# 64-slot experts: the second half of each column block turned by transposes instead of a fold product

## The chip, the cores and the metric

One core of one Trainium2 chip runs the whole kernel. TensorE is called PE here, VectorE DVE, ScalarE ACT, as in the profile's rows; SP issues the loads. The metric is device time in microseconds (us), the median of several runs; beside it stands one profiled execution, from which all rows come.

## The reference

A two-layer decoder trunk on 256 tokens of 1024 channels. Each layer mixes tokens (two attentions) and then channels; the second layer's channel mixer is a top-2-of-8 mixture of experts, and the change lies there:

```python
def _swiglu(x, w1, w3, w2):
    return (jax.nn.silu(x @ w1) * (x @ w3)) @ w2
...
    logits = (xt @ w_router).astype(jnp.float32)
    top_v, top_e = lax.top_k(logits, TOP_K)
    gates = jax.nn.softmax(top_v, axis=-1)
...
    def run(args):
        xb, e = args
        return _swiglu(xb, w1[e], w3[e], w2[e])
```

Everything is float32; w1 and w3 are 1024 x 3584, w2 is 3584 x 1024 for each expert.

## The kernel before

The eight experts are ranked by load and run as four pairs; in each pair one expert gets 128 token slots (large) and one gets 64 (small). Both are worked on in column blocks of the hidden width 3584: three blocks of 1024 columns and one of 512, that is seven parts of 512 columns. `plan` writes the order of steps out by hand. One step is one 1 MB tile of weights. For each block the steps are: w1 of the large, w1 of the small, w3 of the large, w3 of the small expert ("up", 4 steps each, 2 in the block of 512), then w2 ("down") of the block before, small and then large. There are 336 steps, 84 in a pair.

A step passes four engines. SP loads the tile into `raw` (L95, six buffers). ACT casts it to the rounded high part `whi` (L1135, five buffers). DVE subtracts the two to get the low part `wlo` (L1143, four buffers); that frees `raw` for a later load. PE multiplies with both: twelve 512-wide matmuls in a step of a large expert (L119 to L121), eight in one of a small expert (L1080, L1081). `run` casts four steps ahead for `whi` and three for `wlo`. Other work is hung between the steps: `mid[s]` runs before step s's casts, `end[s]` after its matmuls. Each engine works its list in that order.

With 64 slots a small expert would leave half of PE's columns unused, so its two operand parts stand side by side: slots 0 to 63 hold the product with the high part of the tokens, 64 to 127 that with the low part, and the two halves of the result have to be added. The up products of a part stay 128 x 512 in PSUM (`mps`), and `lift` copies them to SBUF (`mh`, four buffers, L1270). Later the part is turned so that the hidden columns become the contraction of w2: `turn_pe` multiplies each 128 x 128 square with `fold`, two identity matrices of 64 on top of each other, which turns it and adds its halves in one product (`ftp`, L1295). `turn_silu` then takes the Silu of the w1 side into `fs` (L1306), `turn_mult` multiplies with the w3 side (L1311), and `turn_small` splits the result into high and low part `sh` (L127, L128). A large expert's part is only turned, with transposes (`htp`, L1299).

The turn of a small expert's block stands after the last w2 step of its block before. In the second, third and fourth pair the work that closes the previous pair falls beside it: `acc_split` (`yh`, `yl`) and `combine`, which scatters the expert's rows back (`cbp`, L1348, L1349) and adds them to `x` (L1352): four parts in a row for the small expert of the previous pair, at the first turn, and spread over several steps for the large one, around the second.

Of the kernel before, what the change touches and what calls it, by code (L numbers as in the profile page):

```python
# [10 lines left out]
F32 = mybir.dt.float32  # L11
# [4 lines left out]
AF = mybir.ActivationFunctionType  # L16
OP = mybir.AluOpType
# [28 lines left out]
LCAP, SCAP = 128, 64  # L46
# [32 lines left out]
class Net:  # L79
# [1205 lines left out]
    def turn_pe(self, hid, turn, bi):  # L1285
        nc = self.nc
        small = self.jobs[self.blocks[bi][0]][2]
        hs = hid.pop(bi)
        turn[bi] = {"ps": []}
        for n in range(self.blocks[bi][2] // 512):  # L1290
            if small:
                ps = self.mmp.tile([128, 2, 4, SCAP], F32, name="ftp", tag="mm")
                for a in range(2):
                    for q in range(4):
                        nc.tensor.matmul(ps[:, a, q, :], hs[a][n][:, q * 128:(q + 1) * 128], self.fold, start=True, stop=True)  # L1295
            else:
                ps = self.mmp.tile([128, 4, 128], F32, name="htp", tag="mm")
                for q in range(4):
                    nc.tensor.transpose(ps[:, q, :], hs[n][:, q * 128:(q + 1) * 128], self.ident)  # L1299
            turn[bi]["ps"].append(ps)  # L1300

    def turn_silu(self, turn, bi):
        turn[bi]["s"] = []
        for ps in turn[bi]["ps"]:
            s = self.mp.tile([128, 4, SCAP], F32, name="fs", bufs=2)
            self.nc.scalar.activation(s, ps[:, 0], AF.Silu)  # L1306
            turn[bi]["s"].append(s)

    def turn_mult(self, turn, bi):
        for s, ps in zip(turn[bi]["s"], turn[bi]["ps"]):  # L1310
            self.nc.vector.tensor_tensor(s, s, ps[:, 1], op=OP.mult)  # L1311

    def turn_small(self, turn, bi):
        hh = self.mp.tile([128, 2, 4, 128], F32R, name="sh")
# [127 lines left out]
```

## Time and profile before

| | us |
|---|---|
| runs | 1671.28, 1671.52, 1675.92 (median 1671.52) |
| the profiled execution | 1670.91 |
| its span, first to last instruction | 1669.1 |
| stretch of the expert stage that the rows cover | 806 to 1637 |
| granted clock of PE, mean over the span | 0.986 |

The profiled execution's own time is 1.8 us above its span. Engine shares of the page are averages over two layers with different limits; what concerns the change is in the expert stage.

### The profile page before, as it was taken

The page shows a single profiled execution, that of the slowest core. Times are in us where ns is not written, and L with a number is a line of the kernel's source. Part 1 is how long each engine was busy: PE and PEld are TensorE (multiplying, and loading weights), DVE is VectorE, ACT ScalarE, POOL GpSimd, SP SyncE. Part 2 cuts the span into 40 slices and gives each one's busy share as a digit, 9 for nine tenths or more (in the row PEclk, how much of TensorE's full clock was granted, in tenths as well). Part 3 has the DMA queues.
Part 4 walks back from the last instruction along what each step waited for, and adds up shares of the span by engine and source line. Part 5 has one row for each costly group of instructions (what it writes and reads, how often), then busy time and mean ns, then how long its engine had stood idle before and what let it go on. Part 6 is the DMA issues. An engine that isn't in the chain of part 4 may idle for free. (4 is left out here: it accounts for less than half of the span.)

```text
span 1669.1 us, 22506 instructions
## 1 busy us (share of the span) xinstructions
PE 1617.4 (97%) x8152; PEld 1343.1 (80%) x8152; DVE 1380.3 (83%) x1686; ACT 1137.4 (68%) x1366; POOL 43.5 (3%) x40
## 2 busy tenths in 40 slices
PE   8899999999989999989999999999999999999996
PEld 7788787888879887878788887888887888878884
DVE  6997777554567668769899899999999999999997
ACT  5546644443436657538787888878887888787874
POOL 0331000000000000000000000000000000000000
PEclk9999999999989999999999999999999999999998
DMA  7533455655536444538999999999999999999993
GB/s 242 180 117 125 157 186 174 211 186 179 182 122 223 137 156 139 195 109 304 400 401 409 398 409 409 403 403 397 408 409 401 403 403 404 409 404 408 406 397 129
DMA packets 171585, 481.26 MB, mean 288 GB/s; under 512 B 8876, under 2 KB 33592, under 8 KB 171464
## 3 DMA queue, kind: packets, MB, share of 16 engines
q1 hardware_dynamic: 170120, 474.98, 75.9%
q0 software_dynamic: 1344, 4.75, 0.9%
q8 instruction: 66, 1.08, 0.3%
q14 instruction: 55, 0.45, 0.1%
HBM read 478.65 MB, written 1.05 MB: 287 GB/s over the span
## 5 line engine op out<-in xcount | busy, mean ns | idle before, releaser
L1143 DVE TENSOR_TENSOR wlo<-raw,whi 128x2048 fp32r<-128x2048 f32 (+1 forms) x338 | 753.4, 2272 | 29.2 <-ACT whi L1135 20.5
L1135 ACT CAST whi<-raw 128x2048 fp32r<-128x2048 f32 (+1 forms) x338 | 637.7, 1905 | 127.4 <-DMA raw<-in_expert_w_dram 57.1
L107 DVE TENSOR_TENSOR wlo<-raw,whi 128x1024 fp32r<-128x1024 f32 (+2 forms) x218 | 254.7, 1190 | 149.0 <-issue 79.0
L105 ACT CAST whi<-raw 128x1024 fp32r<-128x1024 f32 (+2 forms) x222 | 218.4, 1015 | 178.4 <-PE hps L121 51.7
L119 PE MATMUL mps<-wlo,g 128*128 128x512 f32 x448 | 177.8, 397 | 6.8 <-DVE x L1352 3.5
L1080 PE MATMUL mps<-wlo,g 128*128 128x512 f32 x448 | 177.4, 396 | 0.0
L121 PE MATMUL mps<-whi,g 128*128 128x512 f32 x448 | 177.3, 396 | 0.0
L120 PE MATMUL mps<-whi,g 128*128 128x512 f32 x448 | 176.3, 393 | 0.0
L1081 PE MATMUL mps<-whi,g 128*128 128x512 f32 x448 | 175.9, 393 | 0.0
L119 PEld LDWEIGHTS mps<-wlo,g 128*128 128x128 f32 x448 | 84.5, 189 | 27.7 <-DVE x L1352 4.8
L121 PEld LDWEIGHTS mps<-whi,g 128*128 128x128 f32 x448 | 84.4, 188 | 20.2
L120 PEld LDWEIGHTS mps<-whi,g 128*128 128x128 f32 x448 | 84.5, 189 | 19.5
L1080 PEld LDWEIGHTS mps<-wlo,g 128*128 128x128 f32 x448 | 84.1, 188 | 18.7
L1081 PEld LDWEIGHTS mps<-whi,g 128*128 128x128 f32 x448 | 84.1, 188 | 18.6
L402 PE MATMUL dqp<-x,whi 128*128 128x512 f32 x256 | 95.6, 414 | 2.2 <-DVE vm L486 2.2
L119 PE MATMUL macc<-wlo,hi 128*128 128x512 f32 x224 | 89.8, 401 | 0.0
L1080 PE MATMUL macc<-wlo,sh 128*128 128x512 f32 x224 | 88.8, 396 | 0.0
L121 PE MATMUL macc<-whi,lo 128*128 128x512 f32 x224 | 88.3, 394 | 0.0
L1081 PE MATMUL macc<-whi,sh 128*128 128x512 f32 x224 | 87.9, 393 | 0.0
L120 PE MATMUL macc<-whi,hi 128*128 128x512 f32 x224 | 87.9, 392 | 0.0
L119 PE MATMUL hps<-wlo,x 128*128 128x512 f32 (+1 forms) x192 | 71.7, 374 | 0.0
L121 PE MATMUL hps<-whi,x 128*128 128x512 f32 (+1 forms) x192 | 71.3, 372 | 0.0
(373 smaller groups left out, 2942.6 us busy)
## 6 DMA issues: line engine op xcount, KB each, us to landing
raw<-in_expert_w_dram SPq DMA_DIRECT2D x336, 1024.0 KB, 9.5
raw<-in_w_in_dram SPq DMA_DIRECT2D x40, 1024.0 KB, 5.1
raw<-in_dense_w_dram SPq DMA_DIRECT2D x33, 1024.0 KB, 5.0
raw<-in_w_branch_diff_dram SPq DMA_DIRECT2D x8, 1024.0 KB, 4.9
raw<-in_w_out_dram SPq DMA_DIRECT2D x8, 1024.0 KB, 5.0
raw<-in_w_ple_gate_dram SPq DMA_DIRECT2D x8, 1024.0 KB, 5.3
raw<-in_w_branch_mla_dram SPq DMA_DIRECT2D x4, 1024.0 KB, 5.2
raw<-in_w_in_dram SPq DMA_DIRECT2D x4, 768.0 KB, 4.8
```

The source lines that it names most:

```text
L105: self.latest = nc.scalar.copy(hi[:, s], raw[:, s])
L107: nc.vector.tensor_tensor(lo[:, s], raw[:, s], hi[:, s], op=OP.subtract)
L119: mm(ps, sh, ml, start=first, stop=False)
L120: mm(ps, sh, mh, start=False, stop=False)
L121: mm(ps, sl, mh, start=False, stop=last)
L402: mm(*one, start=k == 0 and m == 0, stop=end and m == 1)
L1080: mm(ps, st, ml, start=first, stop=False)
L1081: mm(ps, st, mh, start=False, stop=last)
L1135: self.nc.scalar.copy(hi[:, p], raw[:, p])
L1143: self.nc.vector.tensor_tensor(lo[:, p], raw[:, p], self.his[s][:, p], op=OP.subtract)
```

## The change

Of each block of 1024 columns of a small expert, the first part (n = 0) is turned as before. The second part (n = 1) is turned with eight plain transposes into two PSUM tiles, one for the w1 side and one for the w3 side. The halves are then still apart: ACT copies columns 64 to 127 of each square to SBUF (into the `mh` tile that held the part), DVE adds columns 0 to 63 from PSUM in place, ACT takes the Silu in place, and DVE multiplies the two. The block of 512 has only n = 0. So three of a small expert's seven parts change, twelve in all.

```diff
         for n in range(self.blocks[bi][2] // 512):
-            if small:
+            if small and n == 0:
                 ps = self.mmp.tile([128, 2, 4, SCAP], F32, name="ftp", tag="mm")
...
+                turn[bi]["ps"].append(ps)
             else:
...
+                pss = [self.mmp.tile([128, 4, 128], F32, name="htp", tag="mm") for _ in range(2 if small else 1)]
+                for ps, h in zip(pss, (hs[0][n], hs[1][n]) if small else (hs[n],)):
+                    for q in range(4):
+                        nc.tensor.transpose(ps[:, q, :], h[:, q * 128:(q + 1) * 128], self.ident)
+                turn[bi]["ps"].append(pss if small else pss[0])
+                turn[bi]["h"] = [h[n][:, :4 * SCAP].rearrange("p (a b) -> p a b", a=4) for h in hs] if small else None
...
         for ps in turn[bi]["ps"]:
-            s = self.mp.tile([128, 4, SCAP], F32, name="fs", bufs=2)
-            self.nc.scalar.activation(s, ps[:, 0], AF.Silu)
+            if isinstance(ps, list):
+                for t, p in zip(turn[bi]["h"], ps):
+                    self.nc.scalar.copy(t, p[:, :, SCAP:])
+                    self.nc.vector.tensor_tensor(t, t, p[:, :, :SCAP], op=OP.add)
+                s = turn[bi]["h"][0]
+                self.nc.scalar.activation(s, s, AF.Silu)
+            else:
+                s = self.mp.tile([128, 4, SCAP], F32, name="fs")
+                self.nc.scalar.activation(s, ps[:, 0], AF.Silu)
...
-            self.nc.vector.tensor_tensor(s, s, ps[:, 1], op=OP.mult)
+            self.nc.vector.tensor_tensor(s, s, turn[bi]["h"][1] if isinstance(ps, list) else ps[:, 1], op=OP.mult)
```

The order of instructions shows it at the first turn of the second pair, the place at 1024 to 1041 us of the profile. On PE, between the last w2 step of the small expert and the first of the large one, before:

```order
L1080 MATMUL macc<-wlo,sh 128x512
L1081 MATMUL macc<-whi,sh 128x512
L1295 MATMUL ftp<-fold,mh 128x64 x16
L119 MATMUL macc<-wlo,hi 128x512
L120 MATMUL macc<-whi,hi 128x512
L121 MATMUL macc<-whi,lo 128x512
```

and with the change:

```order
L1080 MATMUL macc<-wlo,sh 128x512
L1081 MATMUL macc<-whi,sh 128x512
L1295 MATMUL ftp<-fold,mh 128x64 x8
L1301 MATMUL htp<-ident,mh 128x128 x8
L119 MATMUL macc<-wlo,hi 128x512
L120 MATMUL macc<-whi,hi 128x512
L121 MATMUL macc<-whi,lo 128x512
```

Half of the fold products are gone and eight transposes follow the others.

On DVE at the same place (`yl` and `x` close the previous pair's small expert), before:

```order
L128 TENSOR_TENSOR yl<-macc,yh 128x512 x2
L1311 TENSOR_TENSOR fs<-fs,ftp 128x256 x2
L1143 TENSOR_TENSOR wlo<-raw,whi 128x2048
L128 TENSOR_TENSOR sh<-fs,sh 128x4x64 x2
L1143 TENSOR_TENSOR wlo<-raw,whi 128x2048
L1352 SCALAR_TENSOR_TENSOR x<-cbp,info,x 128x512 x4
L1143 TENSOR_TENSOR wlo<-raw,whi 128x2048 x12
```

and with the change:

```order
L128 TENSOR_TENSOR yl<-macc,yh 128x512 x2
L1311 TENSOR_TENSOR mh<-mh,htp 128x256 x2
L1321 TENSOR_TENSOR fs<-fs,ftp 128x256
L1321 TENSOR_TENSOR mh<-mh 128x256
L1143 TENSOR_TENSOR wlo<-raw,whi 128x2048
L128 TENSOR_TENSOR sh<-fs,sh 128x4x64
L128 TENSOR_TENSOR sh<-mh,sh 128x4x64
L1143 TENSOR_TENSOR wlo<-raw,whi 128x2048
L1362 SCALAR_TENSOR_TENSOR x<-cbp,info,x 128x512 x4
L1143 TENSOR_TENSOR wlo<-raw,whi 128x2048 x12
```

Two additions into `mh` stand ahead of the products; the subtraction and the four `x` behind them keep their order.

On ACT at the same place, before:

```order
L127 CAST yh<-macc 128x512 x2
L1306 ACTIVATE fs<-ftp 128x256 x2
L1135 CAST whi<-raw 128x2048
L127 CAST sh<-fs 128x4x64 x2
L1135 CAST whi<-raw 128x2048 x5
```

and with the change:

```order
L127 CAST yh<-macc 128x512 x2
L1316 ACTIVATE fs<-ftp 128x256
L1310 COPY mh<-htp 128x256 x2
L1313 ACTIVATE mh<-mh 128x256
L1135 CAST whi<-raw 128x2048
L127 CAST sh<-fs 128x4x64
L127 CAST sh<-mh 128x4x64
L1135 CAST whi<-raw 128x2048 x5
```

Two copies and a Silu in SBUF take the place of the second Silu, ahead of the next `whi` cast.

## Rows read from the trace of the kernel before

**Rows 1.** The page: busy share of PE (part 1); loads with us to landing (part 6).
```profile
PE 1617.4 (97%) x8152; PEld 1343.1 (80%) x8152; DVE 1380.3 (83%) x1686; ACT 1137.4 (68%) x1366; POOL 43.5 (3%) x40
...
raw<-in_expert_w_dram SPq DMA_DIRECT2D x336, 1024.0 KB, 9.5
...
raw<-in_w_out_dram SPq DMA_DIRECT2D x8, 1024.0 KB, 5.0
```

**Rows 2.** Windows: us, busy us of each engine, then PEclk, DMA share, GB/s.
```profile
860.00:920.00 60.00, 60.00 (x282) 49.47 (x281) 56.85 (x35) 48.62 (x36) 0.00 (x0) 1.00 1.03 409
...
925.00:945.00 20.00, 20.00 (x117) 17.37 (x117) 18.56 (x13) 17.22 (x25) 0.00 (x0) 1.00 1.04 389
1042.00:1050.00 8.00, 8.00 (x37) 6.47 (x36) 7.73 (x5) 6.07 (x4) 0.00 (x0) 1.00 1.01 378
1100.00:1118.00 18.00, 18.00 (x80) 14.63 (x79) 17.42 (x13) 13.84 (x10) 0.00 (x0) 1.00 1.01 394
```

**Rows 3.** DMA traffic of the expert stage, 806 to 1637 us.
```profile
DMA packets 95176, 335.78 MB, mean 404 GB/s; under 512 B 5126, under 2 KB 5126, under 8 KB 95121
```

**Rows 4.** Waits of SP's queue from 780 us: in total, times, longest.
```profile
SPq L95 <- DVE wlo L1143: 641.9, 321, 6.4
```

**Rows 5.** Windows of VectorE alone: us, busy us, PEclk, DMA share, GB/s.
```profile
1023.40:1038.20 14.80, 14.79 (x14) 1.00 1.03 410
1052.80:1103.00 50.20, 50.20 (x37) 1.00 1.03 410
```

**Rows 6.** Timeline of VectorE, 1030 to 1046 us: start, us, instruction, count.
```profile
1032.42 0.74 DVE L1311 TENSOR_TENSOR fs<-fs,ftp 128x256 f32<-128x256 f32 x2
1033.08 2.28 DVE L1143 TENSOR_TENSOR wlo<-raw,whi 128x2048 fp32r<-128x2048 f32 x1
...
1038.16 2.72 DVE L1352 SCALAR_TENSOR_TENSOR x<-cbp,info,x 128x512 f32<-128x512 f32 x4
```

**Rows 7.** Timeline of ScalarE: start, us, instruction, in brackets the idle time before it.
```profile
1042.08 1.91 ACT L1135 CAST whi<-raw 128x2048 fp32r<-128x2048 f32 x1 [3.73 <-PE mps L121]
...
1629.28 1.92 ACT L1135 CAST whi<-raw 128x2048 fp32r<-128x2048 f32 x1 [0.67 <-DMA raw<-in_expert_w_dram]
```

**Rows 8.** Timeline of PE, 808 to 828 us.
```profile
810.00 1.03 PE L1299 MATMUL htp<-ident,mh 128*128 128x128 f32 x8
810.79 0.48 PE L1080 MATMUL mps<-wlo,g 128*128 128x512 f32 x1
...
823.42 3.68 PE L1295 MATMUL ftp<-fold,mh 128*128 128x64 f32 x32
826.91 0.48 PE L119 MATMUL mps<-wlo,g 128*128 128x512 f32 x1
```

**Rows 9.** Instructions on tile fs: duration in ns (min/median/max), first and last start.
```profile
L1306 ACT ACTIVATE fs<-ftp x28: 376/384/398, 825.4 to 1631.1; 128x256 f32<-128x256 f32 x28
L1311 DVE TENSOR_TENSOR fs<-fs,ftp x28: 407/414/423, 825.8 to 1631.5; 128x256 f32<-128x256 f32 x28
...
L128 DVE TENSOR_TENSOR sh<-fs,sh x28: 411/418/426, 830.1 to 1634.1; 128x256 fp32r<-128x256 f32 x28
```

**Rows 10.** Waits of PE from 780 us: in total, times, longest.
```profile
PE mps L119 <- DVE x L1352: 3.5, 3, 1.5
```

**Rows 11.** Timeline of VectorE at the first turn of the first pair.
```profile
825.77 0.42 DVE L1311 TENSOR_TENSOR fs<-fs,ftp 128x256 f32<-128x256 f32 x1 [2.47 <-ACT fs L1306]
```

**Rows 12.** Timeline of PE, at 276 and at 1038 us.
```profile
276.63 0.50 PE L119 MATMUL plps<-wlo,x 128*128 128x512 f32 x1 [2.17 <-ACT pr L790]
...
1038.95 0.50 PE L119 MATMUL mps<-wlo,g 128*128 128x512 f32 x1 [1.46 <-DVE x L1352]
```

**Rows 13.** Windows of PE alone: us, busy us (matmuls), PEclk, DMA share, GB/s.
```profile
277.20:280.60 3.40, 3.40 (x10) 0.50 1.00 246
...
816.50:819.90 3.40, 3.40 (x10) 0.50 1.03 408
...
1038.90:1042.40 3.50, 3.45 (x15) 1.00 1.03 411
```

More of the change, by code (lines that the diff above doesn't have):

```diff
@@ L1295, in turn_pe @@
                         nc.tensor.matmul(ps[:, a, q, :], hs[a][n][:, q * 128:(q + 1) * 128], self.fold, start=True, stop=True)
+                turn[bi]["ps"].append(ps)
             else:
[L1297 to L1300, printed above, removed]
+                pss = [self.mmp.tile([128, 4, 128], F32, name="htp", tag="mm") for _ in range(2 if small else 1)]
[4 more added lines that the diff above has]
+                turn[bi]["h"] = [h[n][:, :4 * SCAP].rearrange("p (a b) -> p a b", a=4) for h in hs] if small else None
     def turn_silu(self, turn, bi):
```

## The prediction

> **What bounds the kernel now.** I read the page's busy shares first. PE is busy for 97% of the span [rows 1]. The windows then show a second full resource: in 60 quiet us of the expert stage the loads run at 409 GB/s, and no stretch of the stage reads clearly more [rows 2]. So the first question is which of the two sets the end. Over the whole expert stage, 806 to 1637 us, the mean is 404 GB/s [rows 3], so of these 831 us only 831 x (1 - 404/409) = 10.2 us are not spent at full rate. Some 20 us of each expert pair, where the loads are cut into 2 KB packets, run at 389 GB/s [rows 2] whatever the engines do: 4 x 20 x (1 - 389/409) = 3.9 us. **What faster engines could still win in this stage is therefore about 6 us**, in short dips such as those to 378 and 394 GB/s [rows 2].
>
> A dip comes when a load is issued too late, and a load is issued when a `raw` buffer is free. The waits of the issuing queue name who frees it: VectorE's `wlo` line, 641.9 us in 321 waits [rows 4]. So next I read VectorE. From 1023.4 to 1038.2 it is busy for 14.79 of 14.80 us, and from 1052.8 to 1103.0 for 50.20 of 50.20 [rows 5]: in these two stretches of a pair it has no idle time, and the dips at 1042 and 1100 come with them. The timeline shows what stands between the `wlo` subtractions there, among it the `fs` products and four `x` in a row [rows 6]. Near the end of the stage ScalarE's cast waits for its load again (0.67 us) [rows 7], so the end follows the loads and not the sum of PE's work. PE looks full because it trails the loads by a few us; where it gets ahead, it waits.
>
> **The change part by part.** There are 12 changed parts: 4 small experts with 3 blocks of two parts each, of which the second changes.
>
> *PE.* Two fold products last from 823.42 to 826.91, 3.49 us or 1.74 a part; eight transposes last from 810.00 to 810.79, 0.79 us [rows 8]. A changed part needs eight transposes, so PE gains 1.74 - 0.79 = 0.95 us each, 11.4 us in all. By the first paragraph at most 6 us of this can reach the end, and only where PE is what makes a load late.
>
> *VectorE.* Added are two additions on 128x256 per part. An `fs` product lasts 414 ns [rows 9], and the instruction behind a pair of them starts 0.66 us after the pair (1032.42 to 1033.08) [rows 6]. The product of a changed part reads two operands in SBUF; `sh`, which does so, takes 418 ns [rows 9], so that costs nothing. No row shows an addition with an operand in PSUM that skips every second 64 columns. Its bounds are nothing beyond the product's 0.33 us from start to start, and the whole 0.41 us each: 0.66 to 0.83 us a part. I take 0.66, since in the two full stretches the operands are ready and a pair runs back to back.
>
> The Trainium skill ("Perfetto Trace Analysis", Optimizing Scalar/DVE Operations) speaks against this edit: it gives each VectorE operation on PSUM a fixed 125 ns or so and advises fewer and larger ones. With the 0.96 GHz of "VectorE: DVE Perf Modes" (Specifications) that makes, as an estimate, 392 ns an addition, and the sum below would be 4.3 instead of 3.6 us; the row has 330 ns from start to start, so I stay with the row.
>
> *ScalarE.* Added are two copies of 128x256, by the `fs` Silu 384 ns each [rows 9], and the new Silu waits for the first addition. Queued behind it on ScalarE are the next `whi` casts, for which VectorE's `wlo` and PE wait. VectorE may be inside a `wlo` then, 2.2 us. Behind the first of the full stretches ScalarE stands idle for 3.73 us [rows 7], which hides it; elsewhere a load needs 9.5 us from issue to landing where a load by itself needs 5.0 [rows 1], so the queue covers some 4.5 us of lateness. I cost it at nothing; without this cover it is up to 2.2 us a part.
>
> *Where it lands.* Each pair turns its changed parts at three places. At the third, and at all of the first pair, the queue of loads is deep by the numbers just given, and 0.66 us disappear. In pairs 2 to 4 the first and second place lie in VectorE's full stretches, in which the queue runs nearly dry: 3 x 2 x 0.66 = **+4.0 us** of later issues. I take them whole, since the rate dips there already; the lower bound is nothing. PE's 0.95 us are lost there: PE waits for VectorE's first `x` behind the fold (three times, 3.5 us in all) [rows 10] and will wait longer. One place gains. At the first turn of the first pair VectorE waits 2.47 us for the fold's Silu [rows 11]. Counted from the fold's start, with 0.33 us for each small operation, its last product there ends after 3.49 + 2 x 0.33 = 4.15 us now, and after 1.74 + Silu + copy + two additions + two products = 1.74 + 6 x 0.33 = 3.72 us then: **-0.4 us**.
>
> Sum: 4.0 - 0.4 = +3.6 us on the profiled execution, 1670.9 us, is 1674.5; that execution lies 0.6 us below the median of the runs, 1671.5, so the forecast is **1675 us**. Bounds of this case: half of the delay reaching the end (1673) to the whole of it at 0.83 us (1676). A measurement of this kernel can tell about 0.3%, 5 us, from no change.
>
> **The rivals.**
> *The clock falls while PE waits.* This one ends slower. PE's wait before the first `mps` matmul of a pair was 1.46 us in one case [rows 12] and 3.5 us over three [rows 10], so 1.5, 1.5 and 0.5. With PE 0.95 us earlier and `x` 0.66 us later each grows by 1.61: to 3.1, 3.1 and 2.1. After the wait of 2.17 us that ended at 276.63 [rows 12] the granted clock was 0.50 (1.2 GHz) for 3.4 us; after 1.46 us it stayed at 1.00 (2.4 GHz) [rows 13]. In 3.4 us at 0.50 ten matmuls are counted, in 3.5 us at 1.00 fifteen [rows 13]: a loss of 1.1 us by these counts and of up to 1.7 us by the clock. VectorE's second full stretch begins behind these matmuls, so one to three falls add 1.1 to 5.1 us to the forecast: 1676 to 1680, decided by the second fall. For it: waits as long as one that half clock followed. Against it: that is one row, and the loads' queue may hide part of the loss.
> *The delay is absorbed.* If the queue still covers 0.66 us at the two places, nothing reaches the end: 1671. For it: the rate only dips to 378 GB/s [rows 2], it doesn't stop.
> *PE was the bound.* Its share of 97% [rows 1] says so, and 11.4 us less PE would give 1660; with the loads' room of 6 us, 1665. Against it: the end of the stage waits for loads [rows 7]. The Trainium skill ("Perfetto Trace Analysis", Identifying the Most-Contended Engine, Transposes) says to work on the engine with the highest occupancy first and to use transposes in place of plain matmuls, which is what this change does; the same section calls matmul busy time a poor measure of it.
>
> **How the numbers follow.** Forecast 0.47, clock 0.30, absorbed 0.15, PE 0.05, and 0.03 for additions that count at all twelve places (12 x 0.66 = 7.9 us, 1679). Slower by over 0.3% (above 1676.5): 0.27 of the clock's case, 0.06 of the forecast's, 0.03: 0.36. Faster (below 1666.5): 0.04. Within: 0.60. The range from 1670.5 to 1680 leaves out the PE case, a third of the absorbed one and 0.04 above it, some 0.14.
>
> **What would show it.** Right: PE's fold group shrinks to 4 of 7 parts; VectorE's full stretches in pairs 2 to 4 grow by 0.7 us each and the dips beside them deepen; PE's wait for `x` reaches 2 to 3 us; the granted clock of the windows behind it shows whether it fell. Wrong: the mean rate of the loads over the stage rises above 404 GB/s and the last load lands earlier; then PE stood ahead of VectorE in the chain, and the sum has the wrong sign.

## The result, and the profile after

The changed kernel takes 1680.16 us (median of 9 runs, 1676.37 to 1683.66) against 1671.31 (9 runs): ratio 1.0054, 95% interval 1.0045 to 1.0063, that is **+9.0 us** (7.5 to 10.5). 1675 were forecast, with 1670.5 to 1680 as the range, and the measured time lies just above it; the sign and the kind of the loss were right, its size was not. The profiled execution of the changed kernel has a span of 1681.3 us (before: 1669.1) and lies 2.9 us above the median; its mean granted clock, 0.981, is the lowest of the nine (up to 0.987), so it shows the loss larger than it is in most of them.

The page, parts 1 and 6, answers [rows 1]:

```profile
PE 1615.3 (96%) x8056; PEld 1335.9 (79%) x8056; DVE 1389.0 (83%) x1710; ACT 1144.1 (68%) x1390; POOL 43.5 (3%) x40
...
raw<-in_expert_w_dram SPq DMA_DIRECT2D x336, 1024.0 KB, 10.0
```

PE's busy time fell by only 2.1 us where 11.4 were taken out; half clock, below, is one reason. The windows show where the time went: us, busy us of the five engines, granted clock, DMA share, GB/s. Before:

```profile
820.00:850.00 30.00, 30.00 (x148) 24.96 (x147) 26.14 (x16) 23.89 (x20) 0.00 (x0) 1.00 1.00 385
850.00:1030.00 180.00, 180.00 (x869) 149.15 (x868) 168.91 (x99) 150.75 (x122) 0.00 (x0) 1.00 1.03 406
1030.00:1140.00 110.00, 108.54 (x495) 88.56 (x495) 108.47 (x75) 89.98 (x70) 0.00 (x0) 1.00 1.02 405
...
1250.00:1360.00 110.00, 109.45 (x502) 89.53 (x501) 108.65 (x75) 90.20 (x71) 0.00 (x0) 1.00 1.02 404
...
1470.00:1580.00 110.00, 108.46 (x496) 88.56 (x495) 107.87 (x71) 90.55 (x72) 0.00 (x0) 1.00 1.02 406
```

After, the same steps (the windows of the third and fourth pair follow their steps):

```profile
820.00:850.00 30.00, 29.08 (x139) 23.82 (x139) 25.93 (x18) 24.13 (x22) 0.00 (x0) 1.00 0.96 366
850.00:1030.00 180.00, 177.29 (x839) 145.36 (x838) 169.41 (x102) 149.93 (x125) 0.00 (x0) 1.00 1.03 406
1030.00:1140.00 110.00, 106.86 (x481) 87.10 (x480) 107.94 (x77) 88.96 (x73) 0.00 (x0) 0.98 1.01 390
...
1254.00:1364.00 110.00, 106.73 (x477) 86.98 (x476) 107.58 (x77) 89.02 (x73) 0.00 (x0) 0.98 1.01 394
...
1478.00:1588.00 110.00, 106.86 (x473) 86.89 (x473) 106.63 (x73) 88.66 (x71) 0.00 (x0) 0.97 1.01 393
```

A stretch in which loads run at r instead of 409 GB/s loses its length x (1 - r/409). At the first turn of the first pair (820 to 850 us) that was 1.8 us and is 3.2: +1.4. Over the first and second turn of pairs 2 to 4 (the three windows of 110 us) it was 1.1 + 1.3 + 0.8 = 3.2 and is 5.1 + 4.0 + 4.3 = 13.4: +10.2. Together 11.6 of the 12.2 us between the two spans. The quiet window has 406 GB/s in both. So the time was lost as late loads, at the places the prediction named, and at one that it had as a gain.

What stands at the first turn of the second pair, with the same place of the third and fourth: PE's timeline (start, us, instruction, idle time before it and its end),

```profile
1037.69 0.39 PE L1359 MATMUL cbp<-yl,selt 128*128 128x512 f32 x1
1041.22 0.79 PE L119 MATMUL mps<-wlo,g 128*128 128x512 f32 x1 [3.14 <-DVE x L1362]
1041.81 0.63 PE L120 MATMUL mps<-whi,g 128*128 128x512 f32 x1
...
1262.53 0.50 PE L119 MATMUL mps<-wlo,g 128*128 128x512 f32 x1 [3.27 <-DVE x L1362]
...
1485.99 0.79 PE L119 MATMUL mps<-wlo,g 128*128 128x512 f32 x1 [3.14 <-DVE x L1362]
```

PE's waits in total, times and longest, over the whole trace,

```profile
PE mps L119 <- DVE x L1362: 9.6, 3, 3.3
```

VectorE's timeline,

```profile
1034.03 0.74 DVE L1311 TENSOR_TENSOR mh<-mh,htp 128x256 f32<-128x256 f32 x2
1034.69 0.41 DVE L1321 TENSOR_TENSOR fs<-fs,ftp 128x256 f32<-128x256 f32 x1
```

ScalarE's,

```profile
1045.85 1.91 ACT L1135 CAST whi<-raw 128x2048 fp32r<-128x2048 f32 x1 [4.96 <-PE mps L121]
```

and PE's granted clock behind the three waits (us, busy us and matmuls, clock, DMA share, GB/s):

```profile
1041.12:1044.53 3.41, 3.31 (x8) 0.50 1.00 383
1262.99:1266.40 3.41, 3.41 (x10) 0.50 1.04 413
1484.85:1491.68 6.83, 5.69 (x13) 0.50 1.00 389
```

The additions cost 0.66 us, as priced (1034.03 to 1034.69). PE's wait grew from 1.46 [rows 12] to 3.14 us and from 3.5 [rows 10] to 9.6 over the three. Behind each of the three the granted clock is 0.50 (1.2 GHz), where before it was 1.00 [rows 13]. At the fourth pair's place it is 0.50 for twice as long as at the other two. ScalarE, which the prediction had as cover with 3.73 us of idle time [rows 7], now idles for 4.96: its idle time ends when PE lets go of a `whi` buffer, so it moves with PE and was never slack. VectorE's first wait behind this place names PE as well, and VectorE is what frees `raw` for the loads:

```profile
1048.15 2.29 DVE L1143 TENSOR_TENSOR wlo<-raw,whi 128x2048 fp32r<-128x2048 f32 x1 [0.45 <-PE mps L119]
```

The trace has one more fall of 3.4 us, at 1628 us, behind a wait of 1.90 us for `mh`; before there is none.

### The profile page after: what moved, and what is told of

It is laid out like the page before. It is cut to its first block, busy times and chain, and to the rows that moved or that the text cites. A ratio compares the mean times of both kernels' runs of the same rounds, so it can differ in the third digit from the quotient of the medians.

```text
span 1681.3 us, 22359 instructions
## 1 busy us (share of the span) xinstructions
PE 1615.3 (96%) x8056; PEld 1335.9 (79%) x8056; DVE 1389.0 (83%) x1710; ACT 1144.1 (68%) x1390; POOL 43.5 (3%) x40
## 5 line engine op out<-in xcount | busy, mean ns | idle before, releaser
L119 PE MATMUL mps<-wlo,g 128*128 128x512 f32 x448 | 180.7, 403 | 13.7 <-DVE x L1362 9.6
L1080 PE MATMUL mps<-wlo,g 128*128 128x512 f32 x448 | 178.3, 398 | 0.8 <-DVE wlo L1143 0.8
L121 PEld LDWEIGHTS mps<-whi,g 128*128 128x128 f32 x448 | 85.7, 191 | 20.8
L120 PEld LDWEIGHTS mps<-whi,g 128*128 128x128 f32 x448 | 86.1, 192 | 20.0
L1081 PEld LDWEIGHTS mps<-whi,g 128*128 128x128 f32 x448 | 84.6, 189 | 18.6
```

Of the source, the lines that this page charges most:

```text
L119: mm(ps, sh, ml, start=first, stop=False)
L120: mm(ps, sh, mh, start=False, stop=False)
L121: mm(ps, sl, mh, start=False, stop=last)
L1080: mm(ps, st, ml, start=first, stop=False)
L1081: mm(ps, st, mh, start=False, stop=last)
```

## Experiments

Changes are against the kernel before, in us, from the ratio and its 95% interval (0.1% is 1.67 us). The profiled executions begin the expert stage up to 5 us apart, so rates, waits and distances within that stage are compared, not spans. The diffs are against the changed kernel; those of e3, e7 and e8 against the kernel before.

| | change kept or made | us against before |
|---|---|---|
| the change | all twelve parts | +9.0 (7.5 to 10.5) |
| e1 | first turns of pairs 2 to 4 only | +6.8 (4.5 to 9.4) |
| e2 | all but these | +4.3 (2.8 to 5.8) |
| e9 | first turn of the first pair only | +1.5 (0.0 to 3.0) |
| e10, e15 | second turns only, twice | +3.3 (1.8 to 4.8), 0.0 (-1.7 to 1.7) |
| e11 | third turns only | -0.8 (-2.3 to 0.8) |
| e3 | e1's places, additions alone | +4.5 (2.7 to 6.5) |
| e4 | e1's places, transposes alone | +1.5 (-0.3 to 3.3) |
| e5, e8 | PE kept busy: after, before | +6.8 (4.8 to 8.9), +2.0 (0.0 to 4.0) |
| e6, e7 | `x` one step earlier: after, before | +6.7 (4.5 to 8.9), +1.8 (0.2 to 3.3) |
| e12, e13 | additions on GpSimd; and PE kept busy | +11.9 (9.4 to 14.5), +13.0 (10.9 to 15.2) |
| e14 | e12 at second and third turns only | +3.0 (1.3 to 4.8) |

### Which places

The place is chosen by one condition; here that of the first run (the second has its negation, the others `self.blocks[bi][1] == 1024` and the like).

```diff
-            if small and n == 0:
+            if small and (n == 0 or not (self.blocks[bi][0] >= 2 and self.blocks[bi][1] == 0)):
```

> The change made only at the first turn (first block) of pairs 2 to 4, three of the twelve parts; the other nine keep the fold product. Theory A (the loss is made there: the first x of the previous pair comes later, PE waits about 3.1 us for it instead of 1.5, its clock falls to half for 3.4 us, and the loads behind come later by what PE lost): three parts carry nearly the whole loss, 2.2 to 2.6 us each, 1678 to 1680, with a low window of the granted clock behind each of the three waits. Rival B (the copies and additions cost alike at all twelve places, 9 us / 12 = 0.75 us each): +2.2 us, 1673.5.

> The complement: the change at all places but the first turn of pairs 2 to 4, nine of the twelve parts. Theory A: the three waits for x stay as before the change (1.5, about 0.5 and 1.5 us), no half clock behind them; only the first turn of the first pair costs something (1.5 us of load time in the trace of the changed kernel), so 1671 to 1674. Rival B (alike at all places): 9 x 0.75 = +6.8 us, 1678.

> The change only at the first turn of the first pair, one part of twelve. Theory A (the third PSUM tile of the turn waits for the first addition, so PE gains nothing there, and VectorE's next wlo comes 0.6 us later while the loads' queue is short: 1.5 us of load time lost in the trace of the changed kernel): +1.0 to +1.5 us, 1672. Rival (the lateness of the loads is made up again before the next pair): 1671.

> The change only at the second turns (columns 1024 to 2047) of all four pairs, four parts. VectorE is full there in pairs 2 to 4. Theory A (VectorE's 0.66 us reach the end where it is full): 3 x 0.66 = +2 us, 1673. Rival (PE, which sets the pace there behind its wait for x, gives its 0.95 us back): 1668 to 1671.

> The change only at the third turns (columns 2048 to 3071) of all four pairs, four parts. VectorE has idle time there and the loads' queue is deep. Theory A: 1671, nothing. Rival (the sum of the parts has to give the +4.3 us of the run with nine parts; first pair +1.5 and second turns +2 leave about +1 us for these, since PE then runs ahead into waits): 1672.

> The kernel with the change at the second turns alone once more, for an undisturbed profile. Measured before: +3.3 us where 2.0 were expected. Theory A (VectorE's 0.66 us each in its full stretch): issues of the loads behind the second turns of pairs 2 to 4 come 0.7 us later and stay so, waits for x as before the change. Rival (PE, 0.95 us earlier a pair, waits longer at the next first turn and its clock falls there): waits of over 2 us and a low window behind the first turns of pairs 3 and 4.

Three parts of twelve cost 6.8 us, which falls to theory A; the nine others 4.3, a little above its 1671 to 1674 and well below the rival's 1678. The two sum to 11.1 where the whole costs 9.0, within the intervals. First pair +1.5, as the trace said (its own profile has 371 GB/s from 820 to 850 us, where before has 385); third turns nothing. The second turns gave +3.3 and then 0.0 with the same kernel: they cost between nothing and 3.3 us, and these times don't place it closer. In the profile of the second, the stretch from the first to the last `wlo` of the experts is 3.1 us longer than before, which leans to the former. It shows no wait for `x` longer than the longest before (PE's waits: total, times, longest; the total was 3.5) and no half clock behind them, which speaks against the rival there.

```profile
PE mps L119 <- DVE x L1362: 4.5, 3, 1.5
```

In e1's profile two of the three waits were as long as in the changed kernel, but the clock fell only behind the last. PE's timeline at these two, and windows of PE behind all three (us, busy us, granted clock):

```profile
1039.24 0.50 PE L119 MATMUL mps<-wlo,g 128*128 128x512 f32 x1 [3.12 <-DVE x L1362]
...
1480.66 0.50 PE L119 MATMUL mps<-wlo,g 128*128 128x512 f32 x1 [3.14 <-DVE x L1362]
```

```profile
1039.20:1044.20 5.00, 4.96 (x22) 1.00 0.98 390
1258.30:1263.30 5.00, 4.95 (x21) 1.00 0.98 388
1481.77:1485.19 3.42, 3.42 (x10) 0.50 0.96 380
```

So the fall does not come with every wait of this length. The kernel's times point to the same between executions, though only one of them has a trace: the three with a mean clock of 0.984 to 0.986 took 1673.8 to 1675.0 us, the three with 0.982 or 0.983 took 1679.4 to 1679.7.

e2 was expected to have no half clock, and its profile has one fall, at the first turn of the second pair, which it leaves as it was: PE's wait there is 1.91 us instead of 1.46.

```profile
1040.53 0.50 PE L119 MATMUL mps<-wlo,g 128*128 128x512 f32 x1 [1.91 <-DVE x L1362]
```

```profile
1041.80:1045.20 3.40, 3.40 (x10) 0.50 1.00 400
```

Together these traces give the price of one fall. For each, the starts of the 84 `wlo` of a pair are compared with those in the trace of the kernel before; the table has by how many us the difference grew from the 15th to the 25th, between which the first turn lies (e3 to e5 follow below).

| first turn of pair | 2 | 3 | 4 |
|---|---|---|---|
| the change | 2.2, fall | 2.4, fall | 3.2, fall of 6.8 us |
| e1 | 0.7 | 0.7 | 2.2, fall |
| e2 (place unchanged) | 2.0, fall | 0.0 | 0.0 |
| e3, additions alone | 2.5, fall | 0.9 | 0.9 |
| e4, transposes alone | 0.0 | 0.0 | 0.0 |
| e5, PE kept busy | 0.7 | 0.7 | 0.7 |

Where the clock stays up the change costs VectorE's 0.66 us, even behind a wait of 3.12 us; a fall of 3.4 us adds 1.5 to 2.0. In e1 the two cases stand side by side, at the second pair four `wlo` in a row as before (8.88 us there), at the fourth a break after two:

```profile
1041.07 8.89 DVE L1143 TENSOR_TENSOR wlo<-raw,whi 128x2048 fp32r<-128x2048 f32 x4
...
1482.50 4.48 DVE L1143 TENSOR_TENSOR wlo<-raw,whi 128x2048 fp32r<-128x2048 f32 x2
1487.70 2.29 DVE L1143 TENSOR_TENSOR wlo<-raw,whi 128x2048 fp32r<-128x2048 f32 x1 [0.72 <-ACT whi L1135]
```

### Which half of the change

Additions alone (two on VectorE, the fold products stay), and transposes alone (no copies, no additions):

```diff
+        for t in turn[bi]["h"]:
+            self.nc.vector.tensor_tensor(t, t, turn[bi]["ps"][1][:, 0], op=OP.add)
         for ps in turn[bi]["ps"]:
```

```diff
-                for t, p in zip(turn[bi]["h"], ps):
-                    self.nc.scalar.copy(t, p[:, :, SCAP:])
-                    self.nc.vector.tensor_tensor(t, t, p[:, :, :SCAP], op=OP.add)
-                s = turn[bi]["h"][0]
-                self.nc.scalar.activation(s, s, AF.Silu)
+                s = self.mp.tile([128, 4, SCAP], F32, name="fs", bufs=2)
+                self.nc.scalar.activation(s, ps[0][:, :, :SCAP], AF.Silu)
```

> The kernel before with two additions of 128x256 on VectorE (PSUM operand, in place in mh, result unused) ahead of the products at the first turn of pairs 2 to 4; fold products stay, no copies. The output is the reference's. x comes 0.66 us later at each, PE's waits there grow to about 2.1, 1.2 and 2.2 us. Theory A1 (VectorE's time alone is the cost, the clock does not fall behind 2.1 us): +0.66 x 3 = +2 us, 1673. Theory A2 (2.1 us are enough for the clock to fall): + (0.66 + 1.6) x 2 + 0.7 = +5.2 us, 1676.5. Rival (the additions are hidden): 1671.

> The other half alone at the same three places: eight transposes in place of the second fold product, but no copies and no additions; Silu and product read columns 0 to 63 of each square from PSUM, so the second half of these parts is left out of the result. x stays where it was, PE comes 0.95 us earlier and waits about 2.4, 1.5 and 2.5 us for x. Theory A1 (a wait of that length does not bring half clock): 1671, no change. Theory A2 (it does): +1.6 us at two or three places, +3 to +5 us, 1674.5 to 1676, by PE being faster. Rival C (PE's time counts in this stage after all): -0.95 x 3, 1668.5.

PE's waits for `x`, additions alone and then transposes alone:

```profile
PE mps L119 <- DVE x L1355: 7.0, 3, 2.5
```

```profile
PE mps L119 <- DVE x L1359: 6.4, 3, 2.5
```

The waits with the transposes alone are as worked out (2.49, 1.44 and 2.50 us); with the additions alone they are longer, 2.40, 2.10 and 2.47. With the additions alone the clock fell at one of the three places (window from 1040.8 us, row below; the wait ahead of it was 2.40 us), and the cost lies between A1 and A2; with the transposes alone none came in the profile, and the cost cannot be told from nothing. A faster PE alone brings nothing at these places; VectorE's time costs, and both together make the wait of 3 us, behind which the clock fell at four of five places in the traces of e1 and of the change. The copies on ScalarE have no run of their own; where the clock stays up the whole change costs no more than the additions (table), so they cost nothing at these places.

```profile
1040.80:1044.20 3.40, 3.40 (x10) 0.50 0.90 355
```

### The clock, and the late `x`

PE is kept busy by computing the fourth `cbp` five times; `x` is moved by its step in the plan.

```diff
-            nc.tensor.matmul(ps, st[:, tb * 128:(tb + 1) * 128], yh[:, cs], start=True, stop=False)
-            nc.tensor.matmul(ps, st[:, tb * 128:(tb + 1) * 128], yl[:, cs], start=False, stop=True)
+            for _ in range(5 if self.jobs[m][2] and part == 3 and not done else 1):
+                nc.tensor.matmul(ps, st[:, tb * 128:(tb + 1) * 128], yh[:, cs], start=True, stop=False)
+                nc.tensor.matmul(ps, st[:, tb * 128:(tb + 1) * 128], yl[:, cs], start=False, stop=True)
```

```diff
-                    parts(*[d1 + 2] * 4)
+                    parts(*[d1 + 1] * 4)
```

> The changed kernel, all twelve parts, with the fourth cbp product of the small expert's combine (two matmuls) computed five times instead of once into the same PSUM tile, in pairs 1 to 3's closing: PE works 1.9 us longer while it would wait for the first x, and its wait shrinks from 3.1 to about 1.3 us. VectorE's work and order are unchanged. The result is the same. Theory A (half clock behind the wait is part of the loss, about 1.6 us a place): no low window behind the three waits, 1680 - 3 x 1.6 = 1675. Rival (the fall of the clock costs nothing because the loads' queue covers it; the loss is VectorE's alone): 1680, unchanged; if the extra matmuls delay x: slower than 1680.

> Control for the run in which PE is kept busy: the kernel before with the same repeated fourth cbp product (five times instead of once). Its three waits for x are 1.5, 0.6 and 1.5 us and 1.9 us of extra matmuls cover them, so PE is up to 1.3 us later where the wait was short. Theory A (the repeated matmuls win only what half clock costs, and before has no half clock there): 1671 to 1673, not faster. Rival (repeating matmuls helps for another reason): under 1669.

> The changed kernel with the small expert's combine (cbp on PE, x on VectorE) one step earlier in pairs 2 to 4's start, so that the four x stand ahead of one wlo and the sh work instead of behind. VectorE does the same work. Theory A (the late x is what stops PE): PE's wait for x goes to under 1 us, no half clock behind it, and the loss of the three first turns goes: 1671 to 1674, also since the remaining turns gain nothing. Rival (VectorE's added time itself is the loss, 0.66 us at each place, wherever x stands): no more than the clock's part is won, 1675 to 1680.

> The kernel before with the same earlier combine. Its three waits for x (1.46, 0.55 and 1.54 us) go; there was no half clock behind them. Theory A: a gain of at most these waits, 0 to 3.5 us, 1668 to 1671. Rival (the waits were hidden by the loads' queue): 1671.

The changed kernel with PE kept busy: waits for `x`, and windows of PE behind them.

```profile
PE mps L119 <- DVE x L1363: 4.0, 3, 1.3
```

```profile
1037.20:1042.20 5.00, 5.00 (x22) 1.00 0.97 388
1257.80:1262.80 5.00, 5.00 (x22) 1.00 0.90 352
1480.30:1485.30 5.00, 5.00 (x22) 1.00 0.93 369
```

PE still starts when the first `x` is done, but at full clock. The gain over the changed kernel is 2.2 us, less than the 5 expected. The repeated products cost by themselves, +2.0 in the kernel before, and against that control the change costs 6.8 - 2.0 = 4.8 us instead of 9.0; but the control may take off too much, since in the kernel before they outlast PE's short waits, and here 4.0 us of waiting are left. The earlier `x` gives the same by another way: no wait for `x` is left, it costs 1.8 us by itself (a miss: a gain was expected), and against it the change costs 6.7 - 1.8 = 4.9. **So some 2 to 4 of the 9 us come from the half clock behind PE's wait of about 3 us, and 5 to 7 do not.** Each of these differences has an uncertainty of about 3 us, and both profiles are of the fastest execution of their kernel (1672.8 and 1672.2 us, medians 1676.7 and 1677.2), so whether the clock stayed up in the others isn't shown. In the changed kernel's own trace, by the table, the falls take 2.2 + 2.4 + 3.2 - 3 x 0.66 = 5.8 us, in the execution with the lowest mean clock.

With the earlier `x` the loads still lose time in the three windows (us, busy us of the engines, clock, DMA share, GB/s): VectorE does the same work in the same stretch.

```profile
1030.00:1140.00 110.00, 108.12 (x492) 87.58 (x491) 108.64 (x73) 90.85 (x70) 0.00 (x0) 1.00 1.01 397
1250.00:1360.00 110.00, 107.81 (x490) 87.33 (x489) 108.38 (x73) 90.51 (x70) 0.00 (x0) 1.00 1.01 395
1470.00:1580.00 110.00, 108.38 (x485) 87.10 (x485) 108.53 (x75) 91.14 (x74) 0.00 (x0) 1.00 1.01 399
```

### Additions off VectorE

ScalarE copies the whole transposed part to `mh`, GpSimd adds its halves there; Silu and product of the part come a step later, in `turn_small`.

```diff
-                    self.nc.scalar.copy(t, p[:, :, SCAP:])
-                    self.nc.vector.tensor_tensor(t, t, p[:, :, :SCAP], op=OP.add)
+                    self.nc.scalar.copy(t, p)
+                    self.nc.gpsimd.tensor_tensor(t[:, :, :SCAP], t[:, :, :SCAP], t[:, :, SCAP:], op=OP.add)
```

> The changed kernel, all twelve parts, with the additions taken off VectorE: ScalarE copies the whole transposed part (128x512) from PSUM to mh, GpSimd adds the two halves there (SBUF only), and Silu and product of these parts come one step later. PE's work is that of the changed kernel; VectorE's is that of the kernel before less what the product saves. Theory A (VectorE's 0.66 us at full places and the fall of the clock are the loss): the former goes, the x come 0.66 us earlier again, PE's waits there are about 2.4 us (PE is still 0.95 us early), as in the run with the transposes alone; 1672 to 1675. Rival (it is the longer chain of the turn, copy, addition, Silu, product, that holds ScalarE and VectorE): GpSimd's additions take longer than VectorE's, so 1680 or slower.

> The same with the fourth cbp product computed five times, so that PE doesn't wait long for x. Theory A: both parts of the loss are gone, what remains is the control's +2 us and PE's gain, which doesn't reach the end: 1670 to 1673. Rival (PE's 0.95 us at twelve places reach the end once VectorE is not the limit): 1662 to 1666.

> Transposes and GpSimd additions at the second and third turns only, eight parts; the first turns keep the fold product, so that nothing changes at the waits for x except that PE arrives up to 1.9 us a pair earlier. If PE's gain can reach the end anywhere it is here: -0.95 x 4 at the second turns, where PE sets the pace behind its wait for x, 1666 to 1668. Theory A (the loads are the limit again before the next pair begins): 1669 to 1671.

The first two were a miss, and the rival's side: the additions are slow there, and what waits for them is in the way. GpSimd's group in e12 (busy us, mean ns), the same additions' shortest, median and longest in ns, ScalarE's wait behind them and PE's for `x`, and VectorE's timeline beside an addition:

```profile
L1311 POOL TENSOR_TENSOR mh<-mh 128x256 f32<-128x256 f32 x24 | 46.5, 1956 | 820.9 <-ACT mh L1310 669.3 <-DVE yl L128 96.4 <-DVE x L1365 55.1
```

```profile
L1311 POOL TENSOR_TENSOR mh<-mh x24: 733/2582/2799, 825.0 to 1603.5; 128x256 f32<-128x256 f32 x24
```

```profile
ACT sh L127 <- DVE mh L1328: 17.7, 12, 3.0
```

```profile
PE mps L119 <- DVE x L1365: 11.7, 3, 4.1
```

```profile
1033.10 2.47 DVE L1143 TENSOR_TENSOR wlo<-raw,whi 128x2048 fp32r<-128x2048 f32 x1
1035.50 0.96 DVE L128 TENSOR_TENSOR sh<-fs,sh 128x256 fp32r<-128x256 f32 x1
```

An addition takes 1956 ns on average instead of 414 on VectorE, and the average hides two kinds: 9 of the 24 took 0.73 to 0.92 us, and the 15 that began while a `wlo` was running took 2.3 to 2.8 us, ending about 0.6 us behind that `wlo`. ScalarE, with the casts queued behind, waits 17.7 us for the products; `x` comes later than ever. Keeping PE busy on top of it didn't help: in that trace PE's waits for `x` are still 1.9 to 2.0 us, and the clock fell at the first turns of the second and fourth pair. These runs therefore do not tell what the change would cost without VectorE's 0.66 us, and that question stays with the additions alone (e3).

The last run shows that PE's saving does not reach the end. Up to 1584 us its loads run no faster than before (windows of e14 and of the kernel before), though PE saves 0.95 us at each of eight parts.

```profile
820.00:1584.00 764.00, 754.61 (x3538) 619.36 (x3537) 726.79 (x442) 638.44 (x523) 28.53 (x14) 1.00 1.02 403
```

```profile
820.00:1584.00 764.00, 759.36 (x3594) 626.36 (x3593) 725.59 (x442) 632.49 (x510) 1.09 (x2) 1.00 1.03 404
```

Its +3.0 us come behind that, and a side effect of the edit is the likely cause (it wasn't undone in a run). GpSimd also issues the load of `gb`, which stood alone on its queue at 1403 us; now it stands behind the additions and comes near the end of the stage, as it does in e12 and e13. The clock also fell there, for 6.8 us from 1617.7 us, but of the 3.6 us by which the experts' last `wlo` is late (counted from their first), 2.9 were there before that.

```profile
1590.27 3.53 POOL L1311 TENSOR_TENSOR mh<-mh 128x256 f32<-128x256 f32 x2 [58.35 <-ACT mh L1310]
1593.74 0.55 POOL L324 DMA_DIRECT2D gb<-in_ln_ffn_g_dram  x1
```

No run was measurably faster than the kernel before; the best, third turns only, can't be told from it.

## Why the prediction was wrong

**What bounds the stage: right.** Less PE work brought nothing: third turns alone (3.8 us less of it) -0.8 (-2.3 to 0.8), transposes alone (2.9 us less) +1.5 (-0.3 to 3.3).

**The additions at VectorE's full places: right in price, roughly right in sum.** 0.66 us each was measured, and 4.0 us forecast. At the first turns they reach the loads in full, 3 x 0.66 = 2.0 us by the table; whether the second turns cost their 2.0 isn't settled (0.0 and +3.3 measured). ScalarE's copies, put at nothing, cost nothing at the first turns, though not for the reason given.

**The step that failed: the clock's fall was a rival at 0.30 and should have been the forecast.** Its mechanism was worked out: waits of 3.1, 3.1 and 2.1 us were predicted, 3.14, 3.14 and 3.27 came (the last, at the third pair, a us longer than predicted), and half clock followed each in the profiled execution. The price of one fall was about right as well: 1.5 to 2.0 us by the table, predicted 1.1 to 1.7. The sum had it at nothing, and the trace of the changed kernel lost 5.8 us by it. What held the chance down was that only one row spoke for it, and the sentence that the loads' queue may hide part of the loss. It hid none of the falls in e1 and e3: VectorE's `wlo` stay late by what the fall took. The reading of ScalarE's 3.73 us as cover is of the same kind. The row itself names its end, `<-PE mps`: PE sets the pace there, and what delays PE's first matmul behind `x` comes through. That the clock would fall could not be had from the length of the waits alone: it fell behind 1.91 us in e2 and not behind 3.12 in e1.

**The sign at the first turn of the first pair: wrong,** +1.4 us where -0.4 was worked out. The working counted the chain of operations and forgot PSUM. The kernel has four buffers for such tiles; two hold the `mps` in progress, and a changed turn needs three, not two. PE's third tile waits until VectorE's first addition frees one (read from the trace; no run gave the turn more buffers):

```profile
826.34 0.66 PE L1301 MATMUL htp<-ident,mh 128*128 128x128 f32 x4 [0.92 <-DVE mh L1311]
```

PE saves next to nothing there (the next product starts at 826.75 us, before at 826.91 [rows 8]), and VectorE's next `wlo` starts at 828.49 instead of 827.90. The Trainium skill ("Perfetto Trace Analysis", Optimization Strategy) says that the same gap, repeating on the engine that should be saturated, can mean too little SBUF or PSUM for the next tile. Here it is a single gap of 0.92 us.

With the rival as forecast, 1676 to 1680, and 1.8 us more for the first pair, the sum would have been 1678 to 1682, around the measured 1680. How many falls the median execution had isn't known, so the agreement may be luck.

## What to carry to other kernels

Before an idle time is counted as cover, read what ends it: if it is the engine whose delay is being priced, there is no cover. Count the buffers of each pool that an edit's tiles come from, at each place it stands, since a tile more can give back on the spot what a faster instruction won. When an edit makes one engine early and another late at the same handover, the wait grows by the sum of the two. Such a wait cost nothing more here while the clock stayed up, and 1.5 to 2.0 us where it fell.

## What the hardware showed

- The granted clock does not follow a wait's length alone. It fell to 0.50 (1.2 GHz) behind waits of 3.14, 3.27 and 3.14 us (the change), 2.40 (e3) and 1.91 (e2); it stayed at 1.00 (2.4 GHz) behind 3.12 (e1), 2.47 and 2.10 (e3), 2.49 and 2.50 (e4).
- An addition of 128x256 in SBUF took 0.73 to 0.92 us on GpSimd when no `wlo` was running as it began, and 2.3 to 2.8 us when one was; VectorE's, with one operand in PSUM, took 414 ns. It slowed VectorE too: a `sh` of 418 ns [rows 9] that began beside one took 0.96 us. The Trainium skill ("SBUF — State Buffer", SBUF: two separate sides) has GpSimd and VectorE share a pair of ports that the one that comes first holds for its whole instruction, when VectorE reads two operands from SBUF. `wlo` and `sh` do so, and the rows agree: each of the 15 long additions ended about 0.6 us behind the `wlo` that was running.
